# The head operands of gate and up: split beside the out projection, kept in DRAM, read into the ring

## The chip, the cores and the metric

The kernel runs on one core of a Trainium2 chip. The metric is the device time of one execution in microseconds (us), lower is better; for a kernel it is the median of its runs. TensorE (PE) does the matrix products, VectorE (DVE) and ScalarE (ACT) the elementwise work, GpSimd (POOL) a few powers, and SyncE (SP) issues nearly all transfers, each of them when its own waits have ended and in the order in which they stand in its queue.

## The reference, cut to what matters

```python
mix = jnp.concatenate([a, c], axis=-1) @ w_out[l]       # out projection, 512x2048 @ 2048x2048
x = x + rms_norm(mix, norm_mix_post[l])
hn = rms_norm(x, norm_ffn_pre[l])
f = (jax.nn.silu(hn @ w_gate[l]) * (hn @ w_up[l])) @ w_down[l]   # 2048x5632, twice, and 5632x2048
x = x + rms_norm(f, norm_ffn_post[l])
```

Ahead of it stand the input projection, the attention heads and a short convolution, which the change does not touch. All is float32.

## The kernel before

Each float32 operand of a product is split into two float32r parts, high and low (`split`, L99: ACT casts the high part at L100, DVE subtracts it from the source for the low part at L101). A product is then three matmuls (`mm3`, L122: high by high at L125, high by low at L126, low by high at L127). The parts stand in a ring of four SBUF tiles (`ring_tile`, L85), which are used in turn; a tile can be filled again when all that read it is done.

**Out projection.** The weight comes in chunks of 512 rows by 512 columns (1 MB), each loaded into one of two raw tiles and split into a high and a low part. The last job, `out_last` (L857), keeps four chunks resident, o2_0, o2_1, o3_0 and o3_1 (names by column group and row group), and goes over the four tiles of 128 tokens, `t`, with all four chunks in turn (`n` = 0 to 3). Before the change chunks 0 and 3 stand in the ring and chunks 1 and 2 in the four places x0 to x3. After each column group DVE adds the bank to the sum `m` (L764), ACT squares it (L765), and DVE multiplies by the gain (L766). After a tile's last chunk `residual(t)` (L788) runs as a side generator: the norm, the residual sum `x` in place x4 or x5 (L796), its store to `x1d` (L798), the second norm (L131), four transposes on PE (px, L778), and the split of the result into `acts`. For t of 2 and 3 the sums of a Strassen-like scheme follow (`t1` to `t4`, L247 to L263).

**Gate and up.** They go by quartets `q` of 2048 by 256 weights, alternating gate and up. A quartet takes seven products `i` of 24 matmuls each (128 by 256, 8 blocks by three); product 1 and 2 need the token tiles 0 and 1 only, the others the sums of all four. So the list `order` begins with products 1 and 2 of the first four quartets (HEAD = 4), which can run while the last token tiles are still being normalised: n = 0 to 7 are (0,1), (1,1), (0,2), (1,2), (2,1), (3,1), (2,2), (3,2), and then come products 5, 7, 6, 3, 4 of quartet 0, of quartet 1 and so on. `prepare(n)` (L948) splits the operand of step n into one ring tile, called w; `load_head` (L930) loads the 128 columns that steps of quartets 1, 2 and 3 need into `spare` or `post`, and `load_quartet` (L921) the 256 columns of a whole quartet into the raw tiles or `post` and `pre`. Banks pa, pb and pd hold the products.

A scheduler fixes the order of the instructions on each engine when the program is built; on the chip each engine and SP go through theirs in that order, waiting where a semaphore is not there yet.

Of the kernel before, what the change touches and what calls it, by code (L numbers as in the profile page):

```python
# [11 lines left out]
F32 = mybir.dt.float32  # L12
F32R = mybir.dt.float32r
# [5 lines left out]
P = 128  # L19
D = 2048  # L20
S = 512
NT = S // P
# [33 lines left out]
def trunk(ctx: ExitStack, tc: tile.TileContext, a, out):  # L56
    nc = tc.nc
    w_in, w_out, w_gate, w_up, w_down = (a[n][0] for n in ("w_in", "w_out", "w_gate", "w_up", "w_down"))
    x = a["x"][0]
# [5 lines left out]
    dram = ctx.enter_context(tc.tile_pool(name="dram", bufs=1, space=DRAM))  # L65
    ps = ctx.enter_context(tc.tile_pool(name="ps", bufs=4, space=PSUM))

    def mm_bank(name):
        return ps.tile([P, 512], F32, tag="mm", name=name)
# [15 lines left out]
    def ring_tile(n, m, name, turn=None):  # L85

        i = ring[0] = (ring[0] + 1) % 4
        t = high.tile([P, D + 96], F32R, tag=f"ring{i}", name=name)
        o = {None: 32 * ((i - 1) % 4), "still": 0, "moving": 64 * (i % 2)}[turn]
        return t[:, o : o + n * m].rearrange("p (n m) -> p n m", n=n)  # L90
# [8 lines left out]
    def split(hi, lo, src):  # L99
        nc.scalar.copy(hi, src)  # L100
        nc.vector.tensor_tensor(out=lo, in0=src, in1=hi.bitcast(F32), op=ALU.subtract)  # L101
# [36 lines left out]
    side = []  # L138
# [5 lines left out]
    def side_step():  # L144
        for g in list(side):
            if next(g, done_) is done_:
                side.remove(g)
# [19 lines left out]
    x1d = dram.tile([NT, P, D], F32, name="x1d")  # L167
    hx = dram.tile([2, P, 7, 2, NP, P], F32, name="hx")
    hl = dram.tile([2, P, 4, S], F32, name="hl")
    qkd = {n: dram.tile([NH // 2, 2, P, 2, S], F32, name=f"{n}_parts") for n in ("q", "k")}  # L170
    vd = dram.tile([NH, P, NT, 2, HD], F32, name="v_parts")

# [422 lines left out]
    def place(tag, dtype=F32, shape=(P, D)):  # L595
        count = late["count"] = late.get("count", 0) + 1
        name = f"{tag}_{count}"
        return late["mp" if tag[0] == "m" else "fp"].tile(list(shape), dtype, tag=tag, bufs=1, name=name)
# [142 lines left out]
    def open_ffn(_):  # L741
        while side:
            side_step()
        at.close()
        late["fp"] = ctx.enter_context(tc.tile_pool(name="ffn", bufs=1))
        for n in PLACES:
            place(n)
        late["fp"].tile([P, 512], F32, tag="qd", bufs=1, name="qd")
        late["post"], late["pre"] = place("post"), place("pre")
        for n in ("post", "pre"):  # L750
            w = a["norm_mix_post" if n == "post" else "norm_ffn_pre"]
            nc.sync.dma_start(late[n], w[0:1, :].broadcast_to([P, D]))
        return
        yield

    def two_parts(n):
        return lambda *_: tuple(place(f"x{n + i}", F32R, (P, 4, 512)) for i in range(2))
# [26 lines left out]
    def residual_in(t):  # L784
        late["x", t] = place(f"x{4 + t % 2}")
        nc.sync.dma_start(late["x", t], x[t * P : (t + 1) * P, :])
# [46 lines left out]
    def out_spec(cg, q4, parts=None):  # L833
        return w_out[q4 * 512 : (q4 + 1) * 512, cg * 512 : (cg + 1) * 512], 4, 512, f"o{cg}_{q4}", parts
# [22 lines left out]
    def out_last(ch):  # L857
        for t in range(2):
            residual_in(t)
        for t in range(NT):  # L860
            if t == 2:
                load_quartet(0)
                load_head(1)
            for n in range(4):
                cg, q4 = 2 + n // 2, n % 2
                if q4 == 0:
                    b = mm_bank(f"po_{cg}_{t}")
                out_part(b, t, q4, *ch[n], q4 == 0, q4 == 1)
                if t == NT - 1 and n == 1:
                    for i in range(2):  # L870
                        prepare(i)
                if q4 == 1:
                    evac_mix(cg, t, b)
                if n == 3:
                    side.append(residual(t))
                yield
# [6 lines left out]
    for cg in range(2):  # L883
# [3 lines left out]
                add_job([], open_ffn)  # L887
            job_out(cg, q4, banks, evac_mix)
    add_job(
        [out_spec(2 + n // 2, n % 2, {1: two_parts(0), 2: two_parts(2)}.get(n)) for n in range(4)], out_last, ahead=0  # L890
    )


# [4 lines left out]
    HEAD = 4  # L898
    quartets = [(n // 2, n % 2) for n in range(2 * NC)]
    order = [(q, i) for p in (0, 2) for i in (1, 2) for q in (p, p + 1)]  # L900
    order += [(q, i) for q in range(2 * NC) for i in ((5, 7, 6, 3, 4) if q < HEAD else (1, 5, 7, 2, 6, 3, 4))]
    order[-3:-1] = order[-2:-4:-1]
    raws, heads_raw, operands, psq, tmp, slots = {}, {}, {}, {}, {}, {}

    def slot(kind):

# [10 lines left out]
    def quartet_cols(q, n=256):  # L917
        c, up = quartets[q]
        return (w_up if up else w_gate)[:, c * 256 : c * 256 + n].rearrange("(k p) m -> p k m", p=P)

    def load_quartet(q):  # L921
        if q % 2 == 0:
            r = [wp.tile([P, 8, 256], F32, tag="raw", name=f"raw_q{q}_{i}") for i in range(2)]
        else:
            r = [place(n, F32, (P, 8, 256)) for n in ("post", "pre")]
        for i in range(2):
            nc.sync.dma_start(r[i], quartet_cols(q)[:, 8 * i : 8 * i + 8, :])
        raws[q] = r

    def load_head(q):  # L930
        heads_raw[q] = place("spare" if q % 2 else "post", F32, (P, 16, P))
        nc.sync.dma_start(heads_raw[q], quartet_cols(q, 128))

    def combine(q, s):

        (p11, p21), (p12, p22) = ((r[:, :, :P], r[:, :, P:]) for r in raws[q])
        if s == 1:
            t = slot("s1") if q else place("spare")[:, :1024]
            tmp["s1"] = t.rearrange("p (k m) -> p k m", k=8)
            nc.vector.tensor_add(tmp["s1"], p21, p22)  # L940
        elif s == 3:
            nc.vector.tensor_sub(p21, p11, p21)
        elif s == 2:
            nc.vector.tensor_sub(p21, p22, p21)
        else:
            nc.vector.tensor_sub(p12, p12, p21)

    def prepare(n):  # L948

        if n >= len(order):  # L950
            return prepare_down(n - len(order))
        q, i = order[n]
        if i in (1, 2) and 0 < q < HEAD:
            src = heads_raw[q][:, 8 * (i - 1) : 8 * i, :]
        else:
            (p11, p21), (p12, p22) = ((r[:, :, :P], r[:, :, P:]) for r in raws[q])
            src = {1: p11, 2: p12, 3: p12, 4: p22, 5: tmp.get("s1"), 6: p21, 7: p21}[i]
            if i == 7 and q >= HEAD:
                combine(q, 3)
            if i == (3 if q == last_q else 6):  # L960
                combine(q, 2)
            if i == 3:
                combine(q, 4)
        w = ring_tile(16, P, f"w_{q}_{i}", "still").rearrange("p (a k) m -> p a k m", a=2)
        split(w[:, 0], w[:, 1], src)
        operands[n] = w
        if i == 4:
            if q < last_q - 1:
                load_quartet(q + 2)
            elif q == last_q - 1:  # L970
                for j in (0, 1):
                    load_block(0, j)
                load_block(0, 2)
            else:
                load_block(0, 3)
# [51 lines left out]
    last_q = 2 * NC - 1  # L1027
# [185 lines left out]
                onto(f, u)  # L1213

    def ffn(_):
        ready, ng = 2, len(order)
        for n, (q, i) in enumerate(order):
            product(n)
            yield
            gather(n)  # L1220
            if n == 4:
                load_quartet(1)
            if n == 2 * HEAD - 2:
                combine(0, 1)
                combine(0, 3)
            if q + 1 < HEAD and i in (6, 3):
                combine(q + 1, {6: 1, 3: 3}[i])
            elif q < last_q and i == 3:
                combine(q + 1, 1)
            while ready < n + (3 if n < 2 * HEAD else 4):  # L1230
                prepare(ready)
                ready += 1
            if n in (0, 1):
                load_head(n + 2)
            if i == 7 and q > 0:
                finish(q - 1)
            if i == 6 and q > 0:
                store_h(q - 1)
            if q == last_q:

                for j, t in {1: ((1, 0),), 2: ((1, 1), (2, 0), (2, 1)), 5: ((5, 0),), 3: ((5, 1), (3, 0), (3, 1))}.get(
                    i, ((i, 0), (i, 1))
                ):
                    load_slot(j, 0, (t,))
        finish(last_q)
        store_h(last_q)
        load_block(1, 0)
        for n, (g, cb, i, hf) in enumerate(steps):
            product_down(n)
            yield  # L1250
            gather_down(n)
            while ready < min(ng + n + 4, ng + len(steps)):
                prepare(ready)
                ready += 1
            if cb == 3 and hf == 1:
                load_slot(i, g + 1)
            if g == 2 and cb == 3:
                tail_loads(i, hf)
# [90 lines left out]
```

## Time and profile before

| what | value |
|---|---|
| time, median of three runs | 2063.5 us (2060.89 to 2068.44) |
| the profiled execution, its time | 2065.88 us |
| its span, first to last instruction | 2063.8 us |
| busy: PE, DVE, ACT, POOL | 2010.3, 1713.5, 1008.1, 24.9 us |
| moved by DMA | 346.11 MB, 168 GB/s over the span |
| mean granted TensorE clock | 0.993 |

The span is the time between the first and the last instruction on the core; the execution's time is 2.1 us more than it. Busy times are sums over the whole span. A row of the timeline gives the start in us, the duration, engine, line and operation with out<-in, and in square brackets the idle time of that engine just ahead of the instruction and what ended it. In a table by windows each engine has its busy us and, in brackets, its count of instructions; PEclk is the granted clock of TensorE as a share of full speed.

### The profile page before, as it was taken

The page shows a single profiled execution, that of the slowest core. Times are in us where ns is not written, and L with a number is a line of the kernel's source. Part 1 is how long each engine was busy: PE and PEld are TensorE (multiplying, and loading weights), DVE is VectorE, ACT ScalarE, POOL GpSimd, SP SyncE. Part 2 cuts the span into 40 slices and gives each one's busy share as a digit, 9 for nine tenths or more (in the row PEclk, how much of TensorE's full clock was granted, in tenths as well). Part 3 has the DMA queues.
Part 4 walks back from the last instruction along what each step waited for, and adds up shares of the span by engine and source line. Part 5 has one row for each costly group of instructions (what it writes and reads, how often), then busy time and mean ns, then how long its engine had stood idle before and what let it go on. Part 6 is the DMA issues. An engine that isn't in the chain of part 4 may idle for free.

```text
span 2063.8 us, 37998 instructions
## 1 busy us (share of the span) xinstructions
PE 2010.3 (97%) x16158; PEld 1941.6 (94%) x16158; DVE 1713.5 (83%) x2141; ACT 1008.1 (49%) x1421; POOL 24.9 (1%) x44
## 2 busy tenths in 40 slices
PE   7999999999999998999999999999999999999998
PEld 5899999999788887999999999999999999999996
DVE  6898889887676689989889989989888687878886
ACT  5555454445576464454455545545545344334442
POOL 0000000000000000000000000000000000000000
PEclk9999999999999999999999999999999999999999
DMA  7533333444663643654554545546546937648354
GB/s 247 156 123 99 107 123 121 166 165 145 207 212 102 233 167 108 186 159 139 174 158 150 170 151 166 175 130 189 164 126 194 346 111 255 210 124 304 108 185 154
DMA packets 310026, 346.11 MB, mean 168 GB/s; under 512 B 12985, under 2 KB 271033, under 8 KB 307425
## 3 DMA queue, kind: packets, MB, share of 16 engines
q1 hardware_dynamic: 308544, 338.95, 50.7%
q10 hardware_dynamic: 1312, 4.74, 0.7%
q8 instruction: 126, 2.06, 0.4%
q14 instruction: 44, 0.35, 0.1%
HBM read 283.87 MB, written 62.41 MB: 168 GB/s over the span
## 4 chain that ended last, share of the span: by engine, by line
PE 74%; DVE 13%; DMA 6%; issue 3%; ACT 2%; SPq 1%; POOL 0%; DVEq 0%; POOLq 0%; ACTq 0%
PE pb L127 6%; PE pb L125 6%; PE pb L126 6%; PE pd L126 6%; PE pd L127 6%; PE pd L125 6%; PE pa L125 5%; PE pa L126 5%; PE pa L127 5%; PE pi_b L127 2%; PE pi_b L126 2%; PE pi_b L125 2%; DVE w L101 2%; DVE w_i L101 2%; PE pi_a L127 2%
## 5 line engine op out<-in xcount | busy, mean ns | idle before, releaser
L100 ACT CAST w<-raw_q 128x1024 fp32r<-128x1024 f32 x130 | 136.7, 1052 | 163.3 <-PE pb L127 72.5
L127 PE MATMUL pb<-acts,w 128*128 128x256 f32 x704 | 195.7, 278 | 3.7 <-DVE w L101 3.7
L125 PE MATMUL pb<-acts,w 128*128 128x256 f32 x704 | 195.4, 278 | 1.6 <-ACT w L100 1.6
L127 PE MATMUL pa<-acts,w 128*128 128x256 f32 x704 | 195.0, 277 | 1.9 <-DVE w L101 1.8
L126 PE MATMUL pb<-acts,w 128*128 128x256 f32 x704 | 195.3, 277 | 0.0
L125 PE MATMUL pa<-acts,w 128*128 128x256 f32 x704 | 194.9, 277 | 0.3 <-ACT w L100 0.3
L127 PE MATMUL pb<-x,w 128*128 128x256 f32 x704 | 194.8, 277 | 0.3 <-DVE w L101 0.2
L125 PE MATMUL pb<-x,w 128*128 128x256 f32 x704 | 194.6, 276 | 0.0
L126 PE MATMUL pb<-x,w 128*128 128x256 f32 x704 | 194.6, 276 | 0.0
L126 PE MATMUL pa<-acts,w 128*128 128x256 f32 x704 | 194.5, 276 | 0.0
L126 PE MATMUL pd<-w_d,acts 128*128 128x256 f32 x640 | 179.1, 280 | 3.4 <-DVE w_d L101 3.4
L125 PE MATMUL pd<-w_d,acts 128*128 128x256 f32 x640 | 178.6, 279 | 1.3 <-DMA acts<-hx 1.3
L127 PE MATMUL pd<-w_d,acts 128*128 128x256 f32 x640 | 178.5, 279 | 0.6 <-DMA acts<-hx 0.6
L101 DVE TENSOR_TENSOR w<-raw_q,w 128x1024 fp32r<-128x1024 f32 x130 | 158.1, 1217 | 4.1 <-ACT w L100 4.0
L127 PEld LDWEIGHTS pb<-acts,w 128*128 128x128 f32 x704 | 133.3, 189 | 4.1 <-DVE w L101 4.1
L125 PEld LDWEIGHTS pb<-acts,w 128*128 128x128 f32 x704 | 133.2, 189 | 1.8 <-ACT w L100 1.8
L127 PEld LDWEIGHTS pa<-acts,w 128*128 128x128 f32 x704 | 132.1, 188 | 2.5 <-DVE w L101 2.5
L126 PE MATMUL pd<-w_d,x 128*128 128x256 f32 x480 | 133.5, 278 | 0.0
L125 PE MATMUL pd<-w_d,x 128*128 128x256 f32 x480 | 133.3, 278 | 0.0
L127 PE MATMUL pd<-w_d,x 128*128 128x256 f32 x480 | 133.2, 278 | 0.0
L126 PEld LDWEIGHTS pb<-acts,w 128*128 128x128 f32 x704 | 133.2, 189 | 0.0
L127 PEld LDWEIGHTS pb<-x,w 128*128 128x128 f32 x704 | 132.4, 188 | 0.6 <-DVE w L101 0.6
(322 smaller groups left out, 6895.5 us busy)
## 6 DMA issues: line engine op xcount, KB each, us to landing
raw_q<-in_w_gate SPq DMA_DIRECT2D x44, 1024.0 KB, 5.5
r_i<-in_w_in SPq DMA_DIRECT2D x22, 1024.0 KB, 5.4
raw_i<-in_w_in SPq DMA_DIRECT2D x22, 1024.0 KB, 5.2
post<-in_w_up SPq DMA_DIRECT2D x22, 1024.0 KB, 5.2
pre<-in_w_up SPq DMA_DIRECT2D x22, 1024.0 KB, 5.9
hx<-spare SPq DMA_DIRECT2D x20, 896.0 KB, 8.4
hx<-m SPq DMA_DIRECT2D x20, 896.0 KB, 9.5
raw_o<-in_w_out SPq DMA_DIRECT2D x16, 1024.0 KB, 5.4
```

Of the source, the lines that this page charges most:

```text
L100: nc.scalar.copy(hi, src)
L101: nc.vector.tensor_tensor(out=lo, in0=src, in1=hi.bitcast(F32), op=ALU.subtract)
L125: nc.tensor.matmul(o, lhsT=lhi, rhs=rhi, start=start, stop=False, **kw)
L126: nc.tensor.matmul(o, lhsT=lhi, rhs=rlo, start=False, stop=False, **kw)
L127: nc.tensor.matmul(o, lhsT=llo, rhs=rhi, start=False, stop=stop, **kw)
```

## The change

The products 1 and 2 of the first four quartets no longer have their operands split by `prepare`. A new side generator, `head_operands`, runs beside the last jobs of the out projection: it loads the 128 columns of quartets 0 and 1 into places x0 and x3, splits their halves into x1, x2, x4 and x5, stores each (1 MB, high and low part) to a new DRAM tensor `hw`, and does the same for quartets 2 and 3. `prepare` for these eight steps is then one load from `hw` into the ring tile. Of `out_last`, chunks 0 and 1 now stand in the ring and chunks 2 and 3 in x0 to x3. Quartet 0 is loaded one token tile earlier, and the first four operands are asked for behind chunks 1 and 2 of the last token tile rather than two behind chunk 1.

```diff
+    hw = dram.tile([8, P, 2, 8, P], F32, name="hw")
...
+        side.append(head_operands())
...
+    def head_operands():
+        raw_ = {}
+        def load(q):
+            raw_[q] = place(f"x{3 * (q % 2)}", F32, (P, 16, P))
+            nc.sync.dma_start(raw_[q], quartet_cols(q, 128))
+        load(0)
+        load(1)
+        for _ in range(3):
+            yield
+        for q in range(HEAD):
+            for i in (1, 2):
+                w = place(f"x{(i, 3 + i)[q % 2]}", F32R, (P, 2, 8, P))
+                split(w[:, 0], w[:, 1], raw_[q][:, 8 * (i - 1) : 8 * i, :])
+                nc.sync.dma_start(hw[order.index((q, i))], w.bitcast(F32))
+                if i == 2 and q + 2 < HEAD:
+                    load(q + 2)
+                yield
+                yield
...
 def out_last(ch):
-            if t == 2:
+            if t == 1:
                 load_quartet(0)
-                load_head(1)
...
-                if t == NT - 1 and n == 1:
+                if t == NT - 1 and n in (1, 2):
                     for i in range(2):
-                        prepare(i)
+                        prepare(2 * n - 2 + i)
...
-        [out_spec(2 + n // 2, n % 2, {1: two_parts(0), 2: two_parts(2)}.get(n)) for n in range(4)], out_last, ahead=0
+        [out_spec(2 + n // 2, n % 2, {2: two_parts(0), 3: two_parts(2)}.get(n)) for n in range(4)], out_last, ahead=0
...
-    def load_head(q):
-        heads_raw[q] = place("spare" if q % 2 else "post", F32, (P, 16, P))
-        nc.sync.dma_start(heads_raw[q], quartet_cols(q, 128))
...
 def prepare(n):
-        if i in (1, 2) and 0 < q < HEAD:
-            src = heads_raw[q][:, 8 * (i - 1) : 8 * i, :]
-        else:
+        if i in (1, 2) and q < HEAD:
+            w = operands[n] = ring_tile(16, P, f"w_{q}_{i}", "still").rearrange("p (a k) m -> p a k m", a=2)
+            nc.sync.dma_start(w.bitcast(F32), hw[n])
+            return
...
 def ffn(_):
-        ready, ng = 2, len(order)
+        ready, ng = 4, len(order)
...
-            while ready < n + (3 if n < 2 * HEAD else 4):
+            while ready < n + (5 if ready < 2 * HEAD else 3 if n < 2 * HEAD else 4):
...
-            if n in (0, 1):
-                load_head(n + 2)
```

How the instructions move is shown at three places. In the names the last number only counts allocations; raw_o3_0 is the raw tile of chunk o3_0, x4_26 the place x4 in its 26th allocation.

SP's queue before, from the load of chunk o2_0 to that of quartet 0 (L113 loads a chunk, L786 the residual's input, L932 the head columns, L927 a quartet):

```order
L113 DMA raw_o2_0_7346<-in_w_out 128x4x512
L786 DMA x4_20_7430<-in_x 128x2048
L786 DMA x5_21_7432<-in_x 128x2048
L113 DMA raw_o2_1_7352<-in_w_out 128x4x512
L932 DMA spare_23_7632<-in_w_up 128x16x128
L113 DMA raw_o3_0_7418<-in_w_out 128x4x512
L113 DMA raw_o3_1_7424<-in_w_out 128x4x512
L927 DMA raw_q0_0_7628<-in_w_gate 128x8x256
L927 DMA raw_q0_1_7629<-in_w_gate 128x8x256
```

The same stretch after the change (L763 loads head columns, L773 stores a split operand):

```order
L113 DMA raw_o2_1_7389<-in_w_out 128x4x512
L773 DMA hw_85<-x1_18_7263 128x2048
L773 DMA hw_85<-x2_19_7282 128x2048
L763 DMA x0_20_7286<-in_w_gate 128x16x128
L773 DMA hw_85<-x4_21_7303 128x2048
L773 DMA hw_85<-x5_22_7326 128x2048
L763 DMA x3_23_7330<-in_w_up 128x16x128
L773 DMA hw_85<-x1_24_7345 128x2048
L773 DMA hw_85<-x2_25_7362 128x2048
L773 DMA hw_85<-x4_26_7379 128x2048
L773 DMA hw_85<-x5_27_7410 128x2048
L113 DMA raw_o3_0_7459<-in_w_out 128x4x512
```

All eight stores and two of the four head loads now stand between the load of chunk o2_1 and that of chunk o3_0, where one transfer stood.

DVE before, from the last sum of job (1,1) to the first token tile's second column group (L764 adds a bank, here po_2_0 and po_3_0 of token tile 0; L766 multiplies by the gain):

```order
L764 TENSOR_TENSOR m3_4_5305<-m3_4_5305,po_1_3_0_7333 128x512
L101 TENSOR_TENSOR lo_o3_1_7427<-raw_o3_1_7424,hi_o3_1_7426 128x2048
L766 TENSOR_TENSOR m3_4_5305<-m3_4_5305,post_14_7218 128x512
L764 TENSOR_TENSOR m0_1_5302<-m0_1_5302,po_2_0_7434 128x512
L766 TENSOR_TENSOR m0_1_5302<-m0_1_5302,post_14_7218 128x512
L764 TENSOR_TENSOR m0_1_5302<-m0_1_5302,po_3_0_7462 128x512
```

The same stretch after the change (these two lines are L787 and L789 there):

```order
L787 TENSOR_TENSOR m3_4_5306<-m3_4_5306,po_1_3_0_7366 128x512
L101 TENSOR_TENSOR lo_o2_1_7392<-raw_o2_1_7389,hi_o2_1_7391 128x2048
L789 TENSOR_TENSOR m3_4_5306<-m3_4_5306,post_14_7219 128x512
L787 TENSOR_TENSOR m0_1_5303<-m0_1_5303,po_2_0_7475 128x512
L101 TENSOR_TENSOR x4_26_7379<-x3_23_7330,x4_26_7379 128x1024
L101 TENSOR_TENSOR x5_27_7410<-x3_23_7330,x5_27_7410 128x1024
L789 TENSOR_TENSOR m0_1_5303<-m0_1_5303,post_14_7219 128x512
L101 TENSOR_TENSOR x1_29_7462<-raw_o3_0_7459,x0_28_7461 128x2048
L101 TENSOR_TENSOR x3_31_7468<-raw_o3_1_7465,x2_30_7467 128x2048
L787 TENSOR_TENSOR m0_1_5303<-m0_1_5303,po_3_0_7503 128x512
```

The last two subtracts of the head operands (x4_26 and x5_27, quartet 3) come behind the sum of the first token tile's first bank, and the splits of o3_0 and o3_1 behind those; before the change only the split of o3_1 stood so late, and it stood ahead of that sum.

On PE the twelve matmuls of each chunk follow each other without a break before; after the change the first matmul on the high part of o3_0 (x0_28) stands where it stood, four matmuls of the next token tile come behind it, and then the first on its low part (x1_29).

DVE before, at the end of the last token tile, from its first norm to its second and the sums behind it (w_2_1 is the operand of step (2,1); L258 and L254 are sums of the Strassen-like scheme, L131 the second norm whose result PE transposes into px_3):

```order
L796 SCALAR_TENSOR_TENSOR x5_24_7666<-m3_4_5305,r_mix3_7851,x5_24_7666 128x512 x4
L101 TENSOR_TENSOR x3_26_7896<-m2_3_5304,x2_25_7895 128x1024
L101 TENSOR_TENSOR w_2_1_7962<-post_27_7902,w_2_1_7962 128x1024
L800 TENSOR_REDUCE ssn_3_7863<-ssx_3_7853 128x1
L258 TENSOR_TENSOR m0_1_5302<-m2_3_5304,m0_1_5302 128x1024
L105 TENSOR_SCALAR v_ffn3_7865<-ssn_3_7863 128x1
L101 TENSOR_TENSOR w_2_2_8049<-post_27_7902,w_2_2_8049 128x1024
L131 SCALAR_TENSOR_TENSOR m3_4_5305<-x5_24_7666,r_ffn3_7867,pre_15_7219 128x512 x4
L101 TENSOR_TENSOR acts_72<-px_3_2_7989,acts_72 128x512
L101 TENSOR_TENSOR w_3_1_8005<-spare_28_7936,w_3_1_8005 128x1024
```

The same stretch after the change (L819 is the old L796, L823 L800, L263 L262):

```order
L819 SCALAR_TENSOR_TENSOR x5_35_7705<-m3_4_5306,r_mix3_7892,x5_35_7705 128x512 x4
L101 TENSOR_TENSOR x1_41_8112<-m0_1_5303,x0_40_8111 128x1024
L823 TENSOR_REDUCE ssn_3_7904<-ssx_3_7894 128x1
L263 TENSOR_TENSOR m0_1_5303<-m0_1_5303 128x1024
L105 TENSOR_SCALAR v_ffn3_7906<-ssn_3_7904 128x1
L131 SCALAR_TENSOR_TENSOR m3_4_5306<-x5_35_7705,r_ffn3_7908,pre_15_7220 128x512 x4
L101 TENSOR_TENSOR x5_44_8205<-m0_1_5303,x4_43_8204 128x1024
L101 TENSOR_TENSOR acts_72<-px_3_2_8023,acts_72 128x512
L101 TENSOR_TENSOR acts_72<-px_3_3_8031,acts_72 128x512
L101 TENSOR_TENSOR w_0_5_8145<-spare_42_8142,w_0_5_8145 128x1024
```

The subtracts of w are gone from there, and sums and splits of the scheme, which stood further behind, have moved up into their places.

More of the change, by code (lines that the diff above doesn't have):

```diff
@@ L902, in trunk @@
     order[-3:-1] = order[-2:-4:-1]
-    raws, heads_raw, operands, psq, tmp, slots = {}, {}, {}, {}, {}, {}
+    raws, operands, psq, tmp, slots = {}, {}, {}, {}, {}
     def slot(kind):
@@ L952, in prepare @@
         q, i = order[n]
-        if i in (1, 2) and 0 < q < HEAD:
-            src = heads_raw[q][:, 8 * (i - 1) : 8 * i, :]
-        else:
[L956 to L963, printed above, removed]
+        if i in (1, 2) and q < HEAD:
+            w = operands[n] = ring_tile(16, P, f"w_{q}_{i}", "still").rearrange("p (a k) m -> p a k m", a=2)
+            nc.sync.dma_start(w.bitcast(F32), hw[n])
+            return
+        (p11, p21), (p12, p22) = ((r[:, :, :P], r[:, :, P:]) for r in raws[q])
+        src = {1: p11, 2: p12, 3: p12, 4: p22, 5: tmp.get("s1"), 6: p21, 7: p21}[i]
+        if i == 7 and q >= HEAD:
+            combine(q, 3)
+        if i == (3 if q == last_q else 6):
+            combine(q, 2)
+        if i == 3:
+            combine(q, 4)
         w = ring_tile(16, P, f"w_{q}_{i}", "still").rearrange("p (a k) m -> p a k m", a=2)
```

## Prediction

> **What bounds the kernel now.** I read the page's busy line first, then a table of windows at the seam of out projection and FFN, PE's waits there, and the timelines of all engines and of SP's queue.
>
> ```profile
> PE 2010.3 (97%) x16158; PEld 1941.6 (94%) x16158; DVE 1713.5 (83%) x2141; ACT 1008.1 (49%) x1421; POOL 24.9 (1%) x44
> 760.00:780.00 20.00, 17.84 (x145) 16.79 (x144) 18.64 (x23) 12.19 (x21) 2.63 (x2) 1.00 0.76 241
> 780.00:800.00 20.00, 13.04 (x82) 12.21 (x81) 18.02 (x18) 10.26 (x12) 0.00 (x0) 0.83 0.02 3
> 820.00:840.00 20.00, 20.00 (x179) 20.00 (x178) 19.96 (x25) 10.28 (x10) 0.00 (x0) 1.00 0.62 192
> ```
>
> PE is the bound nearly everywhere; its steady pace is 179 matmuls in 20 us, 0.112 us each. At 780 to 800 it does 82, with DVE at 18.0 of 20 us: this hole, at the FFN's start, is what the change can fill. PE's waits between 763 and 803, and the ends of the stretch from the first head product to the last product of quartet 0:
>
> ```profile
> PE pb L127 <- DVE w L101: 3.7, 2, 3.0
> PE pa L127 <- DVE w L101: 1.8, 2, 1.4
> PE pb L125 <- ACT w L100: 1.6, 1, 1.6
> PE pd L125 <- ACT w L100: 1.6, 1, 1.6
> PE pd L127 <- DVE w L101: 0.8, 1, 0.8
> PE pa L125 <- ACT w L100: 0.3, 1, 0.3
> 753.18 0.28 PE L125 MATMUL pa<-acts,w 128*128 128x256 f32 x1
> ...
> 753.89 0.28 PE L125 MATMUL pa<-acts,w 128*128 128x256 f32 x1
> ...
> 782.69 0.39 PE L125 MATMUL pb<-acts,w 128*128 128x256 f32 x1 [1.63 <-ACT w L100]
> ...
> 786.16 0.58 PE L127 MATMUL pb<-acts,w 128*128 128x256 f32 x1 [2.96 <-DVE w L101]
> 786.00:792.00 6.00, 5.84 (x27) 5.84 (x28) 5.78 (x6) 0.84 (x2) 0.00 (x0) 0.50 0.01 3
> 803.84 0.28 PE L125 MATMUL pb<-x,w 128*128 128x256 f32 x1
> ```
>
> Every wait is for a w that ACT or DVE splits: 9.8 us in all. After the two waits of pb the granted clock is 0.50 for 6 us, in which PE does 27 matmuls instead of 54: 3.0 us. The stretch lasts 803.84 - 753.18 = 50.7 us; its 12 products of 24 matmuls need 32.2 us at steady pace.
>
> **The change, part by part.** (1) *The FFN head.* Eight casts and eight subtracts leave ACT and DVE where DVE is full:
>
> ```profile
> 745.00 1.22 DVE L101 TENSOR_TENSOR w<-raw_q,w 128x1024 fp32r<-128x1024 f32 x1
> 746.13 1.22 DVE L101 TENSOR_TENSOR w<-spare,w 128x1024 fp32r<-128x1024 f32 x1
> 769.12 2.74 DVE L131 SCALAR_TENSOR_TENSOR m<-x,r_ffn,pre 128x512 f32<-128x512 f32 x4 [0.44 <-POOL r_ffn L107]
> 770.07 0.60 PE L778 MATMUL px<-ident,m 128*128 128x128 f32 x4
> 801.14 0.39 PE L127 MATMUL pb<-acts,w 128*128 128x256 f32 x1 [0.75 <-DVE w L101]
> x<-x1d SPq DMA_DIRECT2D x4, 1024.0 KB, 4.8
> ```
>
> Six of the subtracts stand ahead of the 769.12 row (the last token tile's second norm), the first two of them the rows above; back to back each holds DVE 1.13 us, so 6.8 us go, and the two sums that move up ahead of it put 2.3 back: the norm comes at about 764.6, px_3 at 765.5. In the new order PE asks for px_3 right behind four products, at 753.2 + 4 x 24 x 0.118 (their spacing there, six steps from 753.18 to 753.89) = 764.5: a wait of about 1 us, 1.3 with POOL's part. Behind that DVE is ahead of PE up to product 3, whose subtract now stands behind that of product 4: the 0.75 us of the 801.14 row plus one subtract, 1.9. Left in the stretch: 32.2, the four transposes 2.4, the slower spacing of the eight head products 1.2 (192 x 0.006), waits 3.2: 39.0. Gain 50.7 - 39.0 = 11.7 us, the clock dip included. Ends: 14.9 (no wait left at all), and 8 where the reads of w come late. Those reads are 1 MB like the x<-x1d row, 4.8 us; the last three queue on SP behind the store of the last token tile's residual (762 by the shift above), land at 767 to 773 and are wanted at 768.5 to 774: cover about 1 us, so 3 to 4 us could be lost there.
>
> (2) *Chunk o2_1 in the ring.* It now takes the ring pair of job (1,1), which o3_1 took:
>
> ```profile
> 700.76 1.91 ACT L100 CAST hi_o<-raw_o 128x2048 fp32r<-128x2048 f32 x1 [0.25 <-PE po L127]
> 703.33 2.28 DVE L101 TENSOR_TENSOR lo_o<-raw_o,hi_o 128x2048 fp32r<-128x2048 f32 x1
> 703.47 0.39 PE L126 MATMUL po<-x,acts 128*128 128x512 f32 x1
> 711.58 0.39 PE L125 MATMUL po<-hi_o,acts 128*128 128x512 f32 x1
> ```
>
> The pair is free at 700.76; high part 702.7, low part 705.0. PE wants o2_1's low part at 703.47, second chunk of the first token tile; o3_1 had until its fourth. Loss 1.6 us. The chunk ends 11 matmuls later: the rows 703.47 to 711.58 are 36 steps, 0.225 each, so 707.5.
>
> (3) *Chunk o3_0 behind the stores.* This is the term that decides.
>
> ```profile
> 672.14 0.99 SPq L786 DMA_DIRECT2D x<-in_x  x2
> 683.22 0.38 SPq L113 DMA_DIRECT2D raw_o<-in_w_out  x1
> 683.64 0.51 SPq L932 DMA_DIRECT2D spare<-in_w_up  x1
> 692.86 2.57 SPq L113 DMA_DIRECT2D raw_o<-in_w_out  x2
> 711.78 0.69 DVE L764 TENSOR_TENSOR m<-m,po 128x512 f32<-128x512 f32 x1 [3.31 <-PE po L127]
> raw_o<-in_w_out SPq DMA_DIRECT2D x16, 1024.0 KB, 5.4
> spare<-in_w_up SPq DMA_DIRECT2D x2, 1024.0 KB, 9.6
> 676.00:678.00 2.00, 2.00 (x10) 1.65 (x10) 0.97 (x2) 0.72 (x2) 0.00 (x0) 1.00 1.08 421
> ```
>
> SP is strictly in order: it stood still from 673.1 to 683.22 for a raw tile, and issued the load of spare only behind it. Before, o3_0 was asked for at 692.86, 10 us ahead of its use. Now its load stands behind the store of x5_27. That needs the split of quartet 3, whose subtracts DVE does behind the sum of po_2_0, which waits for PE's chunk 2. So: PE 707.5, sum done 708.4 (0.2 after PE as in the 711.78 row, then 0.69), two subtracts 710.7, store issued 710.8, o3_0 issued 711.2. Landing: 716.6 with the 5.4 of a load alone; 720.8 with the 9.6 of one issued close behind another. I take 720.0: x4_26's store of 709.6 and the two behind it are 3.15 MB, at 421 GB/s (a window with the queue full) 7.5 us, and 2.9 us of fixed time (5.4 less 2.5 for 1 MB). It is near the upper end because two stores are still on the way. Cast 1.9: x0_28 is there at 721.9, and PE has stood since 707.5: 14.4 us (10.9 to 15.2). Nothing else stands ahead in PE's order.
>
> The Trainium skill ("DMA: Bandwidth & Descriptors", Queues, rings and completion order) says that the transfers a sequencer issues go through one ring on each engine, consumed in ring order. By that the o3_0 load comes behind both stores, and the sum has the 14.4; were the transfers independent it would have 10.9. The pair at 683 agrees with the first: 9.6 us for the later one.
>
> (4) *Behind that stall.* PE does one matmul and four of the next tile (1.1 us), then wants o3_0's low part, 2.3 us after the high: 1.2 us. And the clock drops: before, the 1.63 and 2.96 us ahead of the rows 782.69 and 786.16 were enough, and here PE stands 14. The cost of the dip is 3.0 us by the rows above, but the wait of 1.2 lies within it, so that both together cost 3.0 (1.2 without a dip).
>
> The same skill ("TensorE: Matmul & The Clock Gate", Part 1) gives about 3.4 us of sustained work until the clock is back; the trace has 6. By the page the dip costs 1.7 instead of 3.0 and the sum falls by 1.3 us.
>
> (5) *Costed at nothing.* The first six head casts and subtracts fill gaps at 681 to 702 (DVE waits 6.75 us ahead of the row below); if that cover were gone they would delay o2_0, wanted at 700.5 and split by 695. The residual input of the first token tile goes out at about 714.5, when x4_26's store is done, instead of 672; behind o3_1 it lands by about 725, and the tile wants it at 714.9 plus the 17 of (2) to (4), 732.
>
> ```profile
> 690.54 2.29 DVE L101 TENSOR_TENSOR x<-raw_o,x 128x2048 fp32r<-128x2048 f32 x1 [6.75 <-ACT x L100]
> 692.75 2.28 DVE L101 TENSOR_TENSOR lo_o<-raw_o,hi_o 128x2048 fp32r<-128x2048 f32 x1
> ...
> 714.93 2.74 DVE L796 SCALAR_TENSOR_TENSOR x<-m,r_mix,x 128x512 f32<-128x512 f32 x4 [0.67 <-POOL r_mix L107]
> ```
>
> **Sum.** 1.6 + 14.4 + 3.0 - 11.7 = +7.3 us. The profiled execution (2065.88) would become 2073.2; it lies 2.4 above the median, so the median goes from 2063.5 to 2070.8. By the ends: 1.6 + 10.9 + 1.2 - 14.9 = -1.2, and 1.6 + 15.2 + 3.0 - 8 = +11.8. About 0.5%, 10.3 us, is what a measurement can tell from no change.
>
> **Rivals.** *Slower, the queue is the bound.* From 668 to 720 SP's queue must move 17 transfers of 1 MB (post, pre, four head loads, o2_0, o2_1, eight stores, o3_0): 17.8 MB, 343 GB/s on average.
>
> ```profile
> 667.00:719.00 52.00, 52.00 (x231) 42.56 (x230) 31.11 (x36) 22.02 (x37) 0.67 (x2) 1.00 0.65 228
> ```
>
> Before, 228 GB/s kept the engines 65% busy there, which is 350 at full; the full windows show 421. At 350 it just suffices; at 320 the load of o3_0 lands 4 us later, and 17.8 MB or the late reads of w in (1) give +11 to +14: 2075 to 2078. It decides from about 325 GB/s down. *Faster, the load of o3_0 is not held up*: if it were issued when its raw tile is free (about 695, the end of o2_0's split, the 692.75 row), it would land by 704 and (3) and (4) vanish: 1.6 - 11.7 = -10.1, 2053.4, and up to 3 less by the upper end of (1). Against it speaks the pair of rows at 683. *The stores do nothing for the head*: if PE waits for reads of w as long as it did for splits, the gain is 3 (the clock dip) and the sum +16, 2079.5; against it, SP may issue the first four reads 5 to 10 us ahead.
>
> **Chances.** Forecast (stall of 11 to 15 us, net -1 to +10.3, with a tail to +11.8) 0.66; queue-bound 0.18; reads late 0.08; load not held up 0.08. Faster by over 0.5%: 0.05 (a good half of the last case); slower: 0.28 (the two slow cases and 0.02 of the tail); within 0.5%: 0.67. The range takes in the lower end -1.2, some scatter of the median (2 us), and most of the queue rival: 2060 to 2079.
>
> **What would show it.** In the profile after: PE idle 13 to 16 us around 708 to 722, ended by ACT's cast of x<-raw_o, SP's load of raw_o issued right behind stores to hw near 711, granted clock 0.50 behind it; the first head product near 771 instead of 753; PE's waits between there and quartet 0's last product below 5 us and no dip there. Wrong would be: raw_o for o3_0 issued before 700, or PE waits on DMA hw of over 3 us.

## The result and the profile after

The changed kernel takes 2073.4 us (median of 8 runs, 2069.59 to 2078.81), the kernel before 2062.7 on the same chip. The ratio is 1.0048, 95% interval 1.0037 to 1.0059, or 9.9 us more (7.6 to 12.2); forecast were 7.3 more. The profiled execution after (2078.81 us, span 2076.7) is the slowest of the eight. Its span is 12.9 us longer than that of before: it is 2.4 us ahead of it at 666 us, loses the 10.6 us found below up to 812 us, and another 4.7 behind 840 us. These 4.7 are not laid to the change: the one large place in them is a wait of 1.8 us for a split operand at 1266.86 with slow matmuls behind it (58 from 1265 to 1275, where the steady pace gives 89), and the run with cheap loads below, which is the same kernel there, has no such wait.

The busy times of the page after differ from those of before by less than 3 us on every engine: the change moves work, it hardly adds any.

PE's waits from 690 to 840 us (in all, times, longest), and then PE's timeline at the places that the prediction named:

```profile
PE po L125 <- issue: 14.3, 1, 14.3
PE px L801 <- DVE m L131: 5.1, 4, 2.1
PE po L126 <- DVE lo_o L101: 1.9, 1, 1.9
PE pd L127 <- DVE w L101: 1.2, 1, 1.2
PE pb L127 <- DVE w L101: 1.0, 1, 1.0
PE po L125 <- ACT hi_o L100: 0.6, 1, 0.6
```

```profile
704.05 0.50 PE L126 MATMUL po<-lo_o,acts 128*128 128x512 f32 x1 [1.93 <-DVE lo_o L101]
...
722.71 0.77 PE L125 MATMUL po<-x,acts 128*128 128x512 f32 x1 [14.29 <-issue]
...
728.48 0.39 PE L125 MATMUL po<-x,acts 128*128 128x512 f32 x1
...
773.42 0.28 PE L125 MATMUL pa<-acts,w 128*128 128x256 f32 x1
...
812.05 0.28 PE L125 MATMUL pb<-x,w 128*128 128x256 f32 x1
```

Of the six rows of waits for w before, two are left, and no wait on a transfer of hw is among them. In their place stands one of 14.3 us. "Issue" only says that PE waited for nothing that the list of waits could name. The timelines of SP, ACT and DVE, in this order, tell what it was.

```profile
699.49 12.28 SPq L773 DMA_DIRECT2D hw<-x  x4
712.11 2.28 SPq L113 DMA_DIRECT2D raw_o<-in_w_out  x2
697.15 2.00 ACT L100 CAST x<-x 128x1024 fp32r<-128x1024 f32 x2 [2.79 <-DMA x<-in_w_gate]
699.68 1.89 ACT L100 CAST hi_o<-raw_o 128x2048 fp32r<-128x2048 f32 x1
706.46 1.99 ACT L100 CAST x<-x 128x1024 fp32r<-128x1024 f32 x2 [3.85 <-DMA x<-in_w_up]
720.72 1.90 ACT L100 CAST x<-raw_o 128x2048 fp32r<-128x2048 f32 x1 [10.75 <-DMA raw_o<-in_w_out]
708.46 0.69 DVE L787 TENSOR_TENSOR m<-m,po 128x512 f32<-128x512 f32 x1 [3.86 <-PE po L127]
709.07 2.35 DVE L101 TENSOR_TENSOR x<-x,x 128x1024 fp32r<-128x1024 f32 x2
```

The chain is the forecast one: PE ends chunk o2_1, DVE adds po_2_0 (708.46) and only then does quartet 3's subtracts (709.07), the last store goes out, SP issues o3_0's load right behind it (712.11), the data is there at 720.7 (8.6 us after the issue), ACT's cast ends at 722.6, PE resumes.

The two profiles are not at the same point here: SP's first load of the FFN's places goes out 2.43 us earlier after.

```profile
667.94 0.34 SPq L752 DMA_DIRECT2D post<-in_norm_mix_post  x1
```

```profile
665.51 0.34 SPq L753 DMA_DIRECT2D post<-in_norm_mix_post  x1
```

With that shift, the first head product (773.42) is 22.7 us later than before, and the last product of quartet 0 (812.05) 10.6 us later. So the out projection lost 22.7, the head won 12.0, and the 10.6 agree with the measured 9.9.

### The profile page after: what moved, and what is told of

The parts are those of the page before. It is cut to its first block, busy times and chain, and to the rows that moved or that the text cites. A ratio compares the mean times of both kernels' runs of the same rounds, so it can differ in the third digit from the quotient of the medians.

```text
span 2076.7 us, 38035 instructions
## 1 busy us (share of the span) xinstructions
PE 2011.0 (97%) x16158; PEld 1942.4 (94%) x16158; DVE 1715.0 (83%) x2141; ACT 1010.8 (49%) x1421; POOL 26.0 (1%) x44
## 4 chain that ended last, share of the span: by engine, by line
PE 64%; DVE 19%; DMA 9%; issue 4%; ACT 3%; SPq 1%; POOL 0%; DVEq 0%; POOLq 0%; ACTq 0%
PE pd L126 6%; PE pd L127 6%; PE pd L125 6%; PE pb L127 5%; PE pb L126 5%; PE pb L125 5%; DVE w L101 4%; PE pa L126 4%; PE pa L127 4%; PE pa L125 4%; DMA raw_q<-in_w_gate 2%; DVE w_i L101 2%; PE pi_b L127 2%; PE pi_b L125 2%; PE pi_b L126 2%
## 5 line engine op out<-in xcount | busy, mean ns | idle before, releaser
L127 PEld LDWEIGHTS pb<-x,w 128*128 128x128 f32 x704 | 132.9, 189 | 2.8 <-DVE w L101 2.8
L127 PEld LDWEIGHTS pb<-acts,w 128*128 128x128 f32 x704 | 132.1, 188 | 1.2 <-DVE w L101 1.2
L126 PEld LDWEIGHTS pb<-x,w 128*128 128x128 f32 x704 | 132.9, 189 | 0.0
L125 PEld LDWEIGHTS pb<-x,w 128*128 128x128 f32 x704 | 132.8, 189 | 0.0
```

Of the source, the lines that this page charges most:

```text
L125: nc.tensor.matmul(o, lhsT=lhi, rhs=rhi, start=start, stop=False, **kw)
L126: nc.tensor.matmul(o, lhsT=lhi, rhs=rlo, start=False, stop=False, **kw)
L127: nc.tensor.matmul(o, lhsT=llo, rhs=rhi, start=False, stop=stop, **kw)
```

## The experiments

The theory: SP's order makes the loss; o3_0's load waits behind stores that wait for DVE, which waits for PE. Its rivals: the transfers' rate, the chunks' new places, or work beside the out projection that was costed at nothing. Differences in us below are ratios times 2062; each run was compared with the kernel before on its own chip.

### Cost and gain apart

**Only the places of the chunks** are changed, in the kernel before:

```diff
-{1: two_parts(0), 2: two_parts(2)}
+{2: two_parts(0), 3: two_parts(2)}
```

> The kernel before with one part of the change alone: chunks 0 and 1 of the last out projection job stand in the ring and chunks 2 and 3 in x0 to x3; no head operands, no stores. If the change of places costs what the trace after shows for chunk o2_1 (PE waits of 2.6 us and a clock dip behind them worth 1.7 us, part of which came from the head casts that are not here), this run is 1 to 4 us above the kernel before: 2064 to 2067, with one PE wait of about 1.6 us for DVE's low part near 705 and no stall of 14 us. The rival, that the change of places itself makes the stall (x0 to x3 too late for o3_0), gives 2075 or more.

Measured: 2062.9, ratio 1.0005 (0.9997 to 1.0014), +1.0 us (-0.6 to 2.9); the time is below the 2064 to 2067 expected. No stall, and the wait of 1.6 us isn't there either: PE does eleven matmuls on the parts of o3_0 (po<-x) ahead of the first on the low part of o2_1.

```profile
704.27 0.39 PE L126 MATMUL po<-x,acts 128*128 128x512 f32 x1
704.51 0.39 PE L126 MATMUL po<-lo_o,acts 128*128 128x512 f32 x1
```

The wait on o2_1 in the changed kernel is thus no price of the places alone. There the matmuls on o3_0 stand behind all of o2_1's, so nothing fills the gap; that this is because o3_0 comes late there is argued, not tried.

**Only the gain**: the kernel before, with the eight operands read ready from DRAM.

```diff
 def prepare(n):
+    if i in (1, 2) and q < HEAD:
+        w = operands[n] = ring_tile(...)
+        nc.sync.dma_start(w.bitcast(F32), <stored parts of q or k>)
+        return
```

(and the same calls of `prepare` and no `load_head`, as in the changed kernel; the values of the eight operands are not the right ones)

> The kernel before with the gain alone: the operands of the first eight products are loaded into the ring from DRAM as in the changed kernel, but from the stored parts of q and k, so that nothing is loaded, split or stored for them beforehand, and the chunks keep their places. What it leaves out: the right values of those eight operands. If the FFN head gains what the trace after shows (50.7 down to 38.6 us from the first head product to the last product of quartet 0), the time is 10 to 13 us below the kernel before: 2050 to 2053. The rival, that the gain needs the stall ahead of it (that a PE which comes 20 us later finds everything ready), gives waits on these loads or on px and a gain of 3 to 7 us: 2056 to 2060.

Measured: 2050.4, ratio 0.9942 (0.9928 to 0.9955), -12.0 us (-14.8 to -9.3). From the first head product to the last product of quartet 0 it takes 38.65 us, as in the changed kernel (38.63):

```profile
753.54 0.28 PE L125 MATMUL pa<-acts,w 128*128 128x256 f32 x1
...
792.19 0.28 PE L125 MATMUL pb<-x,w 128*128 128x256 f32 x1
```

**Only the cost**: `head_operands` and the new places in the kernel before; hw is written and not read, and `prepare` splits as before.

> The kernel before with the cost alone: head operands loaded, split and stored beside the out projection and the chunks in their new places, as in the changed kernel, but the stored parts are not read; the first eight products have their operands split at the FFN's start as before. The result is that of the reference. If cost and gain add up, it is the changed kernel (2073.4) plus the gain of 12: about 2085 (2081 to 2089), 20 to 24 us above the kernel before, with the PE stall of 14 us at 708 to 723 unchanged. If part of the cost comes from the later timing of the changed kernel's own FFN head, it is below 2080.

Measured: 2082.1, ratio 1.0096 (1.0080 to 1.0112), +19.8 us (16.5 to 23.1), just under the expected 20 to 24, with the stall unchanged (14.31 us). Cost and gain add: 19.8 - 12.0 = 7.8 against the measured 9.9, within the intervals.

### Order or rate

**The loads of o3_0 and o3_1 on POOL's queue**, all else as in the changed kernel:

```diff
-        nc.sync.dma_start(raw, ...)
+        (nc.gpsimd if name.startswith("o3_") else nc.sync).dma_start(raw, ...)
```

> The changed kernel with one difference: the loads of chunks o3_0 and o3_1 are issued by POOL's queue instead of SP's, so that they wait for their raw tile alone and not for the stores that stand ahead of them on SP. All bytes are the same. If SP's order is the cause, the load goes out at about 692 to 696 instead of 712, PE's stall falls from 14.3 us to 0 to 6 (what is left is the low part's place x1, whose store lands near 710), and the time from 2073.4 to 2058 to 2064, level with the kernel before or a little below it. If the transfer queue is the bound (1 MB needs 9 to 12 us there whoever issues it, and what is put ahead delays the rest), chunk o3_0 or the head loads behind it land as late as now and the time stays above 2068.

Measured: 2060.0, ratio to before 0.9993 (0.9984 to 1.0001), -1.4 us (-3.3 to 0.2), so 11.3 under the changed kernel by the ratios. In the timelines, POOL's issue of the load, ACT's cast of o3_0, and two waits of PE:

```profile
691.34 0.81 POOL L113 DMA_DIRECT2D raw_o<-in_w_out  x1 [28.86 <-DMA hw<-x]
703.18 1.90 ACT L100 CAST x<-raw_o 128x2048 fp32r<-128x2048 f32 x1 [3.12 <-DMA raw_o<-in_w_out]
705.18 0.77 PE L125 MATMUL po<-x,acts 128*128 128x512 f32 x1 [4.56 <-ACT x L100]
775.55 0.63 PE L801 MATMUL px<-ident,m 128*128 128x128 f32 x4 [3.64 <-DVE m L131]
```

The load goes out 20 us sooner and the stall falls to 4.6, with the same bytes: SP's order made ten of the fourteen. (The bracket of the first row names a store; what the load needs is its raw tile, and DVE's split out of that tile ended at 690.9.) The clock still dips behind the stall, to 0.58 from 708 to 712. And the head now takes 46.05 us (754.88 to 800.93) and not 38.6. Of these 7.4 us more, the transposes of the third token tile, about 2.4 us by the prediction's rows, have only moved into the stretch from ahead of it. The rest is lost: PE reaches the head sooner, DVE does not, the waits in the stretch are 6.1 us instead of 3.1, 3.64 of them for px_3, and the clock is 0.83 from 775 to 785. So about five of the microseconds that the order gave are given back there, and the last product of quartet 0 comes 0.3 us later than before the change.

**Cheap head loads**, in the changed kernel and in the one with POOL's queue: rows in place of columns.

```diff
-            nc.sync.dma_start(raw_[q], quartet_cols(q, 128))
+            nc.sync.dma_start(raw_[q], w_out[P * q : P * q + P, :].rearrange("p (k m) -> p k m", k=16))
```

> The changed kernel, but the four 1 MB loads of the head operands read 128 whole rows of another weight (runs of 8 KB) instead of 128 columns (runs of 512 bytes); same bytes, other values, so the operands of the first eight products are not the right ones. If PE's stall comes from the order on SP and DVE (the last two stores wait for subtracts that stand on DVE behind the sum of po_2_0, which waits for PE at 708.5), the head loads land some 2 to 4 us sooner and nothing follows from it but the small wait for the high part of o2_1: 2070 to 2073, stall still 12 to 14.5 us. If the rate of the transfers sets the stall, 4 MB that go at 400 GB/s instead of 300 end it 3 us or more sooner and the time falls to 2068 or less.

Measured: 2070.0, ratio 1.0038 (1.0023 to 1.0053), +7.8 us. The stall is the same to 0.01 us:

```profile
705.71 2.00 ACT L100 CAST x<-x 128x1024 fp32r<-128x1024 f32 x2 [1.86 <-DMA x<-in_w_out]
722.34 0.76 PE L125 MATMUL po<-x,acts 128*128 128x512 f32 x1 [14.28 <-issue]
```

Quartet 3's cast comes 2.9 us sooner (705.71 against 706.46, in a profile 2.1 us later at that place), and nothing follows for the stall: its subtracts stand behind the sum of po_2_0 all the same. What is gone is the wait of 0.6 us on o2_1's high part and, with it, the slow clock behind chunk o2_1 that cost the changed kernel 1.7 us (shown under the prediction's step 2 below). That is 2.3 us by the traces and 2.1 by the ratios, whose intervals overlap. So the stall of the changed kernel is decided by order, not by rate.

> Both differences: the loads of o3_0 and o3_1 from POOL's queue, and the head operands' loads from whole rows (again not the right values). With SP's order out of the way, what is left of the stall (4.6 us, ended by the landing of o3_0 at 703.2, 11.8 us after its issue) is the transfer queue's. So here the rate should count: o3_0 lands 2 to 4 us sooner, the stall is 0.5 to 2.5 us, and the time 2 to 5 us below the 2060.0 of the run with POOL's queue alone: 2055 to 2058. If the 11.8 us are a fixed delay of that queue, stall and time stay.

Measured: 2059.5, ratio 0.9994 (0.9981 to 1.0007), no better than with POOL's queue alone. The expectation failed: o3_0 lands 12.7 us after its issue (693.73 to 706.40) instead of 11.8, and the stall is 5.6 us. The windows show why the bytes saved no time:

```profile
678.40:684.40 6.00, 6.00 (x28) 4.96 (x27) 4.75 (x4) 6.00 (x7) 0.00 (x0) 1.00 0.63 198
693.80:699.40 5.60, 5.60 (x26) 4.63 (x26) 3.83 (x6) 3.57 (x7) 0.74 (x1) 1.00 1.01 423
699.40:705.40 6.00, 3.44 (x16) 2.51 (x14) 4.77 (x5) 2.41 (x3) 0.00 (x0) 1.00 1.02 427
```

The last two columns are the busy share of the transfer engines and GB/s. The first two head loads are done earlier, and the queue then runs down (198 GB/s) while SP stands at a raw tile; what is asked for behind that, stores above all, fills it at 423 to 427 GB/s while o3_0 is under way. Why it landed even 0.9 us later isn't settled. The Trainium skill ("DMA: Bandwidth & Descriptors", Queues, rings and completion order) says that an engine takes its rings in turn, a packet at a time; by that, rows of 8 KB on SP's ring would leave POOL's ring a smaller share than runs of 512 bytes. No run here separates this.

**The same loads on ACT's queue** instead of POOL's:

> As the run with POOL's queue, but the loads of o3_0 and o3_1 are issued by ACT's queue. If what is left there (11.8 us from issue to landing, a stall of 4.6 us) is the load on the transfer engines, it comes out the same here: landing 11 to 13 us after the issue, stall 4 to 6 us, time 2058 to 2062. If POOL's queue adds a delay of its own, the load lands in 6 to 9 us, the stall is below 2.5 us and the time 2055 to 2058.

Measured: 2062.9, ratio 1.0006 (0.9997 to 1.0015), +1.2 us, which is 0.9 us above the range expected for the time. Landing and stall are as expected, 12.8 us after the issue and 4.8:

```profile
692.55 0.38 ACTq L113 DMA_DIRECT2D raw_o<-in_w_out  x1
705.36 1.90 ACT L100 CAST x<-raw_o 128x2048 fp32r<-128x2048 f32 x1 [3.34 <-DMA raw_o<-in_w_out]
```

So the 12 us are the load on the transfer engines (full at 371 to 388 GB/s in the run with POOL's queue while o3_0 is under way), not POOL's way of issuing.

**No stores**: the eight stores are left out and the ring filled from the stored parts of q and k.

```diff
-                nc.sync.dma_start(hw[order.index((q, i))], w.bitcast(F32))
```

> The changed kernel without the eight stores: the head operands are still loaded and split beside the out projection, but not stored, and the ring is filled from the stored parts of q and k, so that the operands of the first eight products are not the right ones. Loads, splits, places and reads of w are as in the changed kernel. If the cost lies in the stores (their place ahead of o3_0 on SP, and their 8 MB on the queue), o3_0's load goes out at about 692 to 696, the stall is gone (0 to 1 us), and with the head's gain the time is 2050 to 2054. If loads and splits beside the out projection cost PE time of their own (ACT and DVE held by late data), it stays above 2056.

Measured: 2058.0, ratio 0.9984 (0.9974 to 0.9993), -3.3 us (-5.4 to -1.4). The first half holds: o3_0 is issued at 690.51 and cast at 696.09, 5.6 us later, and there is no stall. The time does not: it lies above the 2056 that was set for the other case, loads and splits that cost PE time. The trace bounds that cost. Set on the trace of before by SP's first load as above, the first head product (752.05) is 2.5 us later than before, so that loads, splits and places without the stores cost 2.5 of the 22.7 us; PE waits for px 5.5 us in three, about as in the changed kernel (5.1). The last product of quartet 0 (791.69) is 8.5 us earlier than before. Of these, 2.6 are lost again further on, at three waits on w (3.1 us from 825 to 832, DVE busy without a pause from 826), where neither before nor after has any:

```profile
690.51 0.37 SPq L113 DMA_DIRECT2D raw_o<-in_w_out  x1
696.09 1.92 ACT L100 CAST x<-raw_o 128x2048 fp32r<-128x2048 f32 x1 [0.40 <-DMA raw_o<-in_w_out]
825.95 0.39 PE L127 MATMUL pb<-x,w 128*128 128x256 f32 x1 [1.23 <-DVE w L101]
829.52 0.39 PE L125 MATMUL pd<-x,w 128*128 128x256 f32 x1 [0.80 <-ACT w L100]
831.09 0.38 PE L127 MATMUL pd<-x,w 128*128 128x256 f32 x1 [1.06 <-DVE w L101]
```

Its eleven runs go from 2052.6 to 2060.8, the profiled one at 2054.4; what makes that spread, and so the rest of the difference, stays open.

### Other ways to the gain

**Two quartets**: only quartets 0 and 1 go through hw, 2 and 3 are split at the FFN's start, and the chunks keep their old places.

```diff
-        for q in range(HEAD):
+        for q in range(2):
...
-        if i in (1, 2) and q < HEAD:
+        if i in (1, 2) and q < 2:
```

> Half the change: only quartets 0 and 1 have their operands split ahead and stored (2 loads and 4 stores instead of 4 and 8), quartets 2 and 3 are split at the FFN's start as before, and the chunks keep their old places. By the theory of SP's order no store waits for a late subtract, so there is no stall on o3_0; the head keeps four casts and four subtracts, and its stretch should be 43 to 46 us instead of 50.7 or 38.6: 4 to 7 us gained less about 1 of small waits, 2056 to 2060. If the stores as such cost PE time, it is above 2063.

Measured: 2059.5, ratio 0.9986 (0.9977 to 0.9995), -2.9 us (-4.7 to -1.0): by the interval a little faster than the kernel before. The stores go out by 687, o3_0 right behind its raw tile, and PE has no stall. The head takes 45.9 us; small waits ahead of it cost 2.5 (755.7 with the shift, against 753.18), more than the one expected, and the first read of w is 0.91 late.

```profile
682.36 4.33 SPq L773 DMA_DIRECT2D hw<-x  x4
693.09 2.58 SPq L113 DMA_DIRECT2D raw_o<-in_w_out  x2
753.72 0.35 PE L125 MATMUL pa<-acts,w 128*128 128x256 f32 x1 [0.91 <-DMA w<-hw]
...
799.62 0.28 PE L125 MATMUL pb<-x,w 128*128 128x256 f32 x1
```

In this trace the gain does not last: at the last product of quartet 0 it is 2.2 us ahead of before, and at 842, behind waits for w at 837 and a clock of 0.58 from 838 to 842, it is 0.5 us behind. So the expected time was met, but where the 2.9 us come from is not shown.

**Subtracts on POOL**, in the kernel before, for the second products of quartets 0 to 3:

```diff
-        split(w[:, 0], w[:, 1], src)
+        if n < 8 and i == 2:
+            nc.scalar.copy(w[:, 0], src)
+            nc.gpsimd.tensor_tensor(out=w[:, 1], in0=src, in1=w[:, 0].bitcast(F32), op=ALU.subtract)
```

> The kernel before with another way to relieve DVE: the low parts of the second products of the first four quartets (four subtracts of 128 by 1024) are computed by POOL instead of DVE; nothing is loaded or stored besides. No trace here shows a subtract of that size on POOL. If it takes up to 2.5 us there and does not slow DVE, the head stretch falls from 50.7 to 45 to 48 us and the time to 2057 to 2061; at 4 us or more, or if DVE slows while POOL works, no gain or a loss: 2062 to 2068.

Measured: 2065.0, ratio 1.0007 (0.9997 to 1.0016), no gain; the head takes 55.4 us, 4.7 more than before. The last section shows why.

## Why the prediction was right, and where not

- **(3), the stall, which decided**: 14.4 forecast, 14.29 found, by the forecast mechanism. Both its ends come 3.3 us later than forecast (issue at 712.11 against 711.2 less the shift, 708.8), because o2_1 ended later. Shown by the load on another queue and by the cheap loads.
- **(1), the head**: 11.7 forecast, 12.0 found, and 12.0 in the run with the gain alone. The waits in the stretch are 3.1, forecast 3.2, and the clock dip is gone. That the waits agree is in part luck: forecast were 1.3 for px_3 and 1.9 for the w of product 3, and found were 2.09 and 1.02.

```profile
786.57 1.23 PE L801 MATMUL px<-ident,m 128*128 128x128 f32 x8 [2.09 <-DVE m L131]
809.36 0.38 PE L127 MATMUL pb<-acts,w 128*128 128x256 f32 x1 [1.02 <-DVE w L101]
```

- **(4), behind the stall**: 3.0 forecast. The thirteen matmuls from 722.71 to 728.48 take 5.8 us instead of 2.9: 2.8, near the 3.0 taken from the trace before. The wait for the low part disappears in it, as assumed.
- **(2), chunk o2_1: mis-sized, 1.6 against 4.3.** The waits are 0.64 and 1.93. The first was not forecast: ACT's cast of the high part (699.68) stands behind the cast of quartet 2's columns, which came late (697.15). And a clock dip followed the two waits: the granted clock is 0.57 in the window of 704 to 708, and the eleven matmuls from 704.05 take 4.4 us to the start of the stall (722.71 - 14.29), where eleven steps of 0.225 and the last one's end need 2.7: another 1.7. In the run with cheap loads the first wait is gone and the second is 1.93 too; there the clock stays at 1.00 and the eleven matmuls take 2.8 us. With the cost alone both waits are there (0.71 and 1.93), and so is the dip (0.62 from 700 to 704). The first three rows below are of the changed kernel, the last of the run with cheap loads.

```profile
704.00:708.00 4.00, 3.95 (x10) 3.12 (x11) 0.60 (x1) 1.54 (x2) 0.00 (x0) 0.57 1.01 424
708.00:712.00 4.00, 0.43 (x2) 0.00 (x0) 3.54 (x4) 1.18 (x3) 0.00 (x0) 0.91 0.34 143
724.00:728.00 4.00, 4.00 (x10) 2.80 (x10) 3.23 (x2) 1.32 (x1) 0.00 (x0) 0.50 0.99 398
703.10:708.00 4.90, 2.98 (x12) 1.99 (x11) 2.73 (x2) 2.73 (x4) 0.00 (x0) 1.00 0.95 403
```

- **(5), costed at nothing: wrong by 1.4**, beside the 0.64 above, which is also work of the head's operands in ACT's way. PE's waits for px ahead of the FFN's head are 3.0 us after and were 1.6 before, here from the lists of waits of after and of before; what makes them longer was not tried:

```profile
PE px L801 <- DVE m L131: 3.0, 3, 1.2
```

```profile
PE px L778 <- DVE m L131: 1.6, 4, 0.9
```

- **The sum**: 4.3 + 14.3 + 2.8 + 1.4 - 12.0 = 10.8, against 10.6 from the rows and 9.9 from the runs. The step that failed most is (2), by 2.7 us: 1.7 for the slow clock behind the waits, which the prediction counted in (4) but not here, 0.6 for the cast that came late, and 0.3 for the wait itself.
- **The rivals.** Reads of w late: no such wait after. Load not held up: it was, to 712.11. Queue-bound: the window of 667 to 719, moved by the shift and in the table below, has 97% busy engines and 322 GB/s, just under the 325 at which that rival was said to decide. That sign was not a good one: the engines idle at the place that counts (143 GB/s from 708 to 712, the row above), and cheap loads left the stall at 14.28. With the order taken away the rate is next: 4.6 us of stall.

```profile
664.60:716.60 52.00, 41.25 (x174) 32.90 (x172) 30.54 (x31) 22.08 (x31) 0.00 (x0) 0.92 0.97 322
```

## What to carry to other kernels

A load that is issued in order behind stores waits for whatever these wait for, down to the engine that waits for the load: before adding stores to a queue, look up which load stands next and by when it is wanted, and give the two different queues. When the order is mended, expect the next limit (here the transfers' rate, 4.6 us, and DVE at the head) to take back part of it. Look at the clock behind each wait of a microsecond or two: here a wait of 1.93 us alone cost nothing more, and with one of 0.64 just ahead of it another 1.7 us.

## What the runs showed of the hardware

**POOL and DVE stop each other.** POOL's subtract of 128 by 1024 takes 2.8 to 3.4 us (DVE's 1.22), and while it runs DVE's instructions on two SBUF operands last about as long as POOL's. The run with subtracts on POOL, POOL first, then DVE:

```profile
753.60 2.92 POOL L967 TENSOR_TENSOR w<-raw_q,w 128x1024 fp32r<-128x1024 f32 x1 [5.65 <-ACT w L966]
756.49 3.40 POOL L967 TENSOR_TENSOR w<-spare,w 128x1024 fp32r<-128x1024 f32 x1
754.29 3.32 DVE L254 TENSOR_TENSOR m<-m 128x1024 f32<-128x1024 f32 x1
757.53 2.91 DVE L766 TENSOR_TENSOR m<-m,post 128x512 f32<-128x512 f32 x1
771.13 6.97 DVE L131 SCALAR_TENSOR_TENSOR m<-x,r_ffn,pre 128x512 f32<-128x512 f32 x4 [0.45 <-POOL r_ffn L107]
```

Before, the first is 1.22, the second 0.68 and the four of the last 2.74 us. Four subtracts of 1.2 us were taken from DVE, and 8.6 us put on it by these three rows. The Trainium skill ("SBUF — State Buffer", SBUF: two separate sides) says that the two hold a shared port pair for a whole instruction each, DVE when it has two SBUF inputs; the trace agrees.

**The time of the same 1 MB load went by the load on the transfer engines more than by the queue**: from issue to cast, o3_0 takes 5.6 us from SP's queue without the stores, 8.6 from SP's queue in the changed kernel, where the engines had run down to 143 GB/s when it was issued, and 11.8, 12.7 and 12.8 from POOL's queue (twice) and ACT's, beside the stores.
